# Chunks 3 to 10 of the gelu up-projections as seven block products, with weight sums on VectorE and the residual spilled

## The chip, the cores and the metric

The kernel runs on one core of a Trainium2 chip, as one launch. The metric is the device time of one execution in microseconds; less is better. The engines are TensorE (PE, with its weight loads listed as PEld), VectorE (DVE), ScalarE (ACT), GpSimd (POOL) and SyncE (SP); each works through its own queue.

## The reference, cut to what matters

Two layers, each a token mixer (attention, then a gated recurrence) and a gated feed-forward network, with an RMS norm before and after each and the result added to the residual. The sequence has 512 tokens, the model 1024 features, the feed-forward network 3072. All tensors are float32. The change concerns the up-projection below.

```python
def conv_ffn(x, w_up, conv_w, conv_b, w_down):
    u = causal_dwconv(x @ w_up, conv_w, conv_b)     # width 3 along the tokens
    g, v = u[..., :D_FF], u[..., D_FF:]
    return (jax.nn.gelu(g, approximate=True) * v) @ w_down

x = x + rms_norm(h, norm_mix_post[layer])
h = rms_norm(x, norm_ffn_pre[layer])
h = conv_ffn(h, ffn_w_up[layer], ...)
x = x + rms_norm(h, norm_ffn_post[layer])
```

## The kernel before

Precision comes from splitting. Each float32 operand is held as two fp32r tiles, `hi` (a rounded copy) and `lo` (what is left over), and a product is three matmul passes: hi with hi, hi with lo, lo with hi (`mm3`, L257). `split` (L148) makes them: ScalarE copies `raw` into `hi`, then VectorE subtracts `hi` from `raw` into `lo`. The activations of a stage lie feature by token in `hT`, a pair of tiles of 128 partitions x 8 feature blocks x 512 tokens.

Weights come through a planner written out by hand. `plan` lists every weight block in the order of use. `load` (L193) has SyncE fetch one block of 1 MB into one of three `raw` buffers; `pump` (L167) cuts a block into two units of 128 output features, splits each in two steps of 512 columns, and stops when eight units are live; `take` hands a unit to the matmuls and `done` releases it. `tick` (L222), called after every tile, lets waiting side work go on and then calls `pump`, with a limit of one unit when six or more are live. Loads are issued only when no cut pieces are left.

The feed-forward network (`ffn`, L591) runs over 12 chunks `j`. A chunk is 256 gelu features and the 256 value features that go with them, four tiles of 128 features x 512 tokens. A tile is 8 feature blocks x 3 passes = 24 matmuls of 512 columns into one PSUM bank (`feat_tiles`, `feat`); chunk 0 runs in halves of 256 tokens, because the last tokens come out of the norm late. Each tile goes to `sink` (L607): `conv` (L594) has ScalarE multiply and add the bias from PSUM, VectorE add the two shifted terms, and then ScalarE does the gelu, or VectorE the product with the gelu tile. The 24 gelu tiles stay in the general pool of 32 tiles of 512 columns (`gen`, L118) until the down-projection (`rows_proj`) splits them as activations.

All engines issue in the order in which the program emits the instructions (L102). So an instruction that waits holds up everything emitted behind it on its engine. Dependencies between engines are found by the framework from the tiles; PSUM tiles are one bank each, eight of them (`psum`, L121).

The residual lies in `x_sb`, 128 partitions x 4 token tiles x 1024, from the first load to the end. The norms at the end of a stage (`postnorm`, `prenorm`) read it and write it; during the 12 chunks of a feed-forward network nothing touches it. `gain` (L133) loads a gain row over all partitions into one of two buffers, on GpSimd's queue.

## Time and profile before

| | us |
|---|---|
| median of three runs | 1455.94 (1455.89 to 1456.03) |
| span of the profiled execution | 1454.0 |
| VectorE busy | 879.8 |
| ScalarE busy | 675.9 |
| first feed-forward network, chunks after the norms of the stage before | 510.5 to 764.3 |
| second feed-forward network, the same | 1063.0 to 1316.8 |

The time of a run is the device's own for the whole execution; the span goes from the first to the last instruction of the one execution that was profiled. In a row of instructions the first number after the bar is the busy time of the group and the second the mean of one in ns, then comes the idle time of the engine just ahead of them and what ended it. Matmuls overlap one another, so the duration of one is longer than the distance to the next. In a row of the chain or the timeline the first number is the start and the second the length. In a row of a stretch come the busy times of PE, PEld, DVE, ACT and POOL with their instruction counts, then the granted clock of TensorE, the share of the DMA engines and the GB/s.

### The profile page before, as it was taken

What the parts mean: (1) busy time and instruction counts of PE and PEld (TensorE: products, weight loads), DVE (VectorE), ACT (ScalarE), POOL (GpSimd) and SP (SyncE); (2) the same over time, 40 slices, a digit from 0 to 9 for tenths busy, and PEclk for the clock granted to TensorE, in tenths of its full rate; (3) what the DMA queues carried; (4) which work ended last, traced back from release to release, by engine and by line L of the source; (5) the groups of instructions that cost most, each with busy time, mean ns of one, the idle gap of its engine ahead of it and who ended that gap; (6) DMA issues with size and microseconds to landing.
All of it is one profiled execution on the core that took longest, in us unless ns stands there. A gap on an engine that the chain in (4) does not pass through costs nothing.

```text
span 1454.0 us, 18793 instructions
## 1 busy us (share of the span) xinstructions
PE 1445.0 (99%) x6861; PEld 1214.4 (84%) x6861; DVE 879.8 (61%) x1955; ACT 675.9 (46%) x1532; POOL 133.9 (9%) x275
## 2 busy tenths in 40 slices
PE   9999999999999999999999999999999999999998
PEld 7888888888888898888888888888898888888886
DVE  6767747474735975555564338769775555564333
ACT  7656636262615553343444335589453434444221
POOL 0340414040402100000000001000100000000000
PEclk9999999999999999999999999999999999999999
DMA  7653637372726343323323322432333233223201
GB/s 225 207 146 109 174 113 208 104 215 97 216 96 211 102 131 100 103 87 102 101 88 116 115 73 88 131 116 84 120 102 116 87 102 102 87 104 128 88 0 58
DMA packets 125364, 172.76 MB, mean 119 GB/s; under 512 B 8736, under 2 KB 102392, under 8 KB 125272
## 3 DMA queue, kind: packets, MB, share of 16 engines
q1 hardware_dynamic: 114280, 145.48, 31.0%
q0 software_dynamic: 10144, 25.04, 5.9%
q8 instruction: 54, 0.88, 0.2%
q10 hardware_dynamic: 848, 1.05, 0.2%
q14 instruction: 38, 0.31, 0.1%
HBM read 156.24 MB, written 15.29 MB: 118 GB/s over the span
## 4 chain that ended last, share of the span: by engine, by line
PE 93%; ACT 4%; DVE 3%; issue 1%; DVEq 0%; ACTq 0%
PE ps L259 55%; PE acc L259 24%; PE v L758 8%; PE v L688 1%; DVE xb L967 1%; PE O L909 1%; PE S L854 1%; PE S L808 1%; DVE wlo L150 1%; ACT sig L988 1%; ACT whi L149 1%; PE O L259 1%; PE tr L341 1%; ACT sig L1007 0%; ACT a L1005 0%
## 5 line engine op out<-in xcount | busy, mean ns | idle before, releaser
L259 PE MATMUL ps<-hT,whi 128*128 128x512 f32 (+1 forms) x2752 | 801.3, 375 | 0.0
L259 PEld LDWEIGHTS ps<-hT,whi 128*128 128x128 f32 x2752 | 503.6, 188 | 91.6
L259 PE MATMUL ps<-hT,wlo 128*128 128x512 f32 (+1 forms) x1376 | 515.3, 374 | 0.0
L150 DVE TENSOR_TENSOR wlo<-raw,whi 128x512 fp32r<-128x512 f32 x360 | 230.8, 686 | 187.2 <-ACT whi L149 187.1
L259 PEld LDWEIGHTS ps<-hT,wlo 128*128 128x128 f32 x1376 | 259.1, 188 | 46.5
L149 ACT ACTIVATE whi<-raw 128x512 fp32r<-128x512 f32 x360 | 204.6, 621 | 135.4 <-PE acc L259 121.0
L600 DVE SCALAR_TENSOR_TENSOR u<-ps,cols,u 128x511 f32<-128x511 f32 x192 | 143.8, 749 | 140.6 <-ACT u L596 137.2
L259 PE MATMUL acc<-whi,ahi 128*128 128x512 f32 x512 | 199.7, 390 | 0.0
L259 PE MATMUL acc<-whi,alo 128*128 128x512 f32 x512 | 199.4, 389 | 0.1
L259 PE MATMUL acc<-wlo,ahi 128*128 128x512 f32 x512 | 199.3, 389 | 0.0
L143 ACT ACTIVATE whi<-raw,first_w 128x128 fp32r<-128x128 f32 (+1 forms) x432 | 146.2, 425 | 56.6 <-PE ps L259 33.9
L596 ACT ACTIVATE u<-ps,cols 128x512 f32<-128x512 f32 x96 | 74.8, 779 | 210.0 <-PE ps L259 210.0
L144 DVE SCALAR_TENSOR_TENSOR wlo<-raw,first_w,whi 128x128 fp32r<-128x128 f32 (+1 forms) x432 | 139.5, 389 | 1.4 <-ACT whi L143 1.3
L259 PEld LDWEIGHTS acc<-whi,alo 128*128 128x128 f32 x512 | 96.1, 188 | 20.5 <-DVE alo L150 0.5
L259 PEld LDWEIGHTS acc<-whi,ahi 128*128 128x128 f32 x512 | 96.1, 188 | 19.8
L259 PEld LDWEIGHTS acc<-wlo,ahi 128*128 128x128 f32 x512 | 96.2, 188 | 19.8
L758 PE MATMUL v<-whi,hT 128*128 128x512 f32 x320 | 102.4, 393 | 0.0
L302 POOL DMA_DIRECT2D turned<-T x36 | 19.6, 547 | 763.4 <-DVE T L296 759.9
L309 POOL DMA_DIRECT2D ft<-turned x144 | 78.7, 554 | 39.6 <-issue 17.7
L758 PEld LDWEIGHTS v<-whi,hT 128*128 128x128 f32 x320 | 60.1, 188 | 12.3
L611 ACT ACTIVATE u<-u 128x512 f32<-128x512 f32 x48 | 30.3, 632 | 80.4 <-DVE u L600 80.4
L758 PE MATMUL v<-wlo,hT 128*128 128x512 f32 x160 | 62.3, 389 | 0.0
(171 smaller groups left out, 1010.7 us busy)
## 6 DMA issues: line engine op xcount, KB each, us to landing
raw<-in_ffn_w_up_dram SPq DMA_DIRECT2D x48, 1024.0 KB
raw<-in_attn_w_qkv_dram SPq DMA_DIRECT2D x67, 512.0 KB
raw<-in_ffn_w_down_dram SPq DMA_DIRECT2D x24, 1024.0 KB
raw<-in_lru_w_in_dram SPq DMA_DIRECT2D x8, 1024.0 KB
turned<-T POOLq DMA_DIRECT2D x28, 256.0 KB, 2.6
ft<-turned POOLq DMA_DIRECT2D x112, 64.0 KB, 5.8
vrows<-v SPq DMA_DIRECT2D x16, 256.0 KB
vp<-vrows SPq DMA_DIRECT2D x16, 256.0 KB
```

Source lines behind the costliest of these rows:

```text
L143: nc.scalar.activation(hi[:, k], raw[:, k], AF.Copy, scale=w)
L144: nc.vector.scalar_tensor_tensor(lo[:, k], raw[:, k], w, hi[:, k].bitcast(F32), op0=ALU.mult, op1=ALU.subtract)
L149: nc.scalar.activation(hi, raw, AF.Copy)
L150: nc.vector.tensor_tensor(lo, raw, hi.bitcast(F32), op=ALU.subtract)
L259: mm(dst, l[a], r[b], start=start and n == 0, stop=stop and n == 2)
L302: nc.gpsimd.dma_start(d, T)
L309: nc.gpsimd.dma_start(t[32 * c : 32 * c + 32].rearrange("j (b x) -> j b x", b=4), d.rearrange("(b j) (c x) -> c j b x", j=32, c=4)[c],)
L341: nc.tensor.transpose(ps[:, k * P : (k + 1) * P], xs[i][:, k * P : (k + 1) * P], ident)
L596: nc.scalar.activation(u, ps, AF.Identity, scale=cc[:, j : j + 1], bias=cc[:, 48 + j : 49 + j])
L600: nc.vector.scalar_tensor_tensor(u[:, d:], ps[:, : S - d], wc, u[:, d:], op0=ALU.mult, op1=ALU.add)
L611: nc.scalar.activation(u, u, AF.Gelu_apprx_tanh)
L758: mm(banks[t], hT[a][:, k, t * P : (t + 1) * P], W[b][:, k % 2, :], start=(k, a, b) == (0, 0, 0), stop=(k, a, b) == (KD - 1, 1, 0),)
```

## The change

In chunks 3 to 10 of both networks the gelu half, a product of 256 output features x 1024 inputs x 512 tokens, is cut in two along each of outputs, inputs and tokens, and done as seven products of half-size blocks instead of eight (Strassen's scheme in Winograd's form). A block product is 128 features x 512 inputs x 256 tokens: 4 feature blocks x 3 passes = 12 matmuls of 256 columns. The sums that the scheme needs are made in four places.

- **Weights.** `w_cols` marks these blocks as `wino`. Instead of two units of 128 features, `summed` makes four units from one raw block, the sums being made in place in `raw` by VectorE (four of 512 columns), the splits being one of 1024 columns for the first three units and one of 512 for the fourth. `pump` takes the gelu and the value block together: one sum, first half of the value block, the four summed units, second half of the value block.
- **Tokens.** `token_sums` runs as side work from chunk 1 on, once per network. GpSimd adds `hi` and `lo` back together for the blocks it needs, VectorE forms four sums, each is split. The eight kept tiles lie in the residual's tile, in the two gain buffers and in four general tiles.
- **Residual.** `token_sums` first sends `x_sb` to DRAM on GpSimd's queue; `x_back` fetches it into the same place at chunk 11.
- **Products.** `seven` runs the seven products (steps 1 to 7) and eight quarters of the two value tiles (a to h, six matmuls of 512 columns each) in the order `5 a 1 3 b c 6 2 d 7 e f 4 g h`. Two PSUM banks hold the running sums in their first 256 columns. ScalarE copies product 5 and the sum after product 3 to SBUF and writes the negative of product 1 over the second bank; VectorE makes the other token half of each output tile by a subtraction into the bank's last 256 columns, after 6 and after 7. `tick` is called after each of the 15 steps.

```diff
+SEVEN = range(3, 11)
-    x_sb = cp.tile([P, 4, D], F32, tag="x_sb", name="x_sb")
+    X = [cp.tile([P, 4, D], F32, tag="x_sb", name="x_sb")]
...
+    def summed(i, raw):
+        a, b, c, d = (raw[:, 4 * k : 4 * k + 4, m * P : m * P + P] for m, k in ((0, 0), (0, 1), (1, 0), (1, 1)))
+        shape = [KD, P]
+        def first(hi, lo):
+            two = [h.rearrange("p (k m) c -> p k (m c)", m=2) for h in (hi, lo)]
+            split(*two, raw[:, 0:4, :])
+            nc.vector.tensor_tensor(a, a, c, op=ALU.add)
+        def second(hi, lo):
+            split(hi, lo, raw[:, :, 0:P])
+            nc.vector.tensor_tensor(b, a, b, op=ALU.add)
+            nc.vector.tensor_tensor(a, a, d, op=ALU.subtract)
+        def third(hi, lo):
+            split(hi, lo, raw[:, :, 0:P])
+        def fourth(hi, lo):
+            split(hi[:, 0:4], lo[:, 0:4], d)
+        def ahead():
+            nc.vector.tensor_tensor(c, c, d, op=ALU.add)
+        return [(None, None, ahead)] + [((i, n), shape, f) for n, f in enumerate((first, second, third, fourth))]
...
     def pump(limit=2):
...
+            if not pieces and i + (i < len(plan) and plan[i][0] == "wino") < state["dma"]:
+                if plan[i][0] == "wino":
+                    (s1, *u), v = summed(i, raws.pop(i)), [
+                        plain(i + 1, j, r) for j, r in enumerate(parts_of("feat", raws.pop(i + 1)))
+                    ]
+                    pieces.extend([s1, v[0], *u, v[1]])
+                    state["cv"] += 2
...
+            while pieces and pieces[0][0] is None:
+                pieces.pop(0)[2]()
...
         for j in range(12):
+            if j == 1:
+                side(token_sums(hT, T))
             if j == 11:
+                x_back()
                 prep(3)
+            if j in SEVEN:
+                seven(hT, T, lambda b, ps: sink(b, ps, j))
+            else:
+                feat_tiles(2, hT, lambda b, ps: sink(b, ps, j), j == 0)
...
+    def x_back():
+        X[0] = cp.tile([P, 4, D], F32, tag="x_sb", name=nm("x_sb"))
+        nc.gpsimd.dma_start(X[0], kept.pop())
...
+    def token_sums(hT, T):
+        d = dp.tile([P, 4, D], F32, name=nm("x_kept"))
+        nc.gpsimd.dma_start(d, X[0])
...
+        yield 1
+        def both(k0, n):
+            o = gen(s="B").rearrange("p (k t) -> p k t", k=2)
+            hi, lo = (h[:, k0 : k0 + 2, n * 256 : n * 256 + 256] for h in hT)
+            nc.gpsimd.tensor_tensor(o, hi.bitcast(F32), lo.bitcast(F32), op=ALU.add)
+            return o
...
+        yield 2
+        for k in range(2):
+            b11, b12, b22, b21 = (B[k, n] for n in ((0, 0), (0, 1), (1, 1), (1, 0)))
+            tt(b11, b11, b12, op=ALU.subtract)
+            tt(b12, b12, b22, op=ALU.subtract)
+            tt(b22, b22, b11, op=ALU.add)
+            tt(b21, b21, b22, op=ALU.subtract)
+            yield 1
+            for n, b in enumerate((b11, b22, b12, b21)):
+                split(homes[2 * n][k], homes[2 * n + 1][k], b)
...
+    def seven(hT, T, sink):
+        i, iv = chunk(), chunk()
+        t = gen(s="part")
...
+        left = {
+            1: (0, pairs(0), block(0, 0), 0), 5: (0, pairs(1), turn(0), 1), 6: (1, row(0), turn(1), 1),
+            2: (1, row(4), block(1, 0), 0), 7: (2, row(0), turn(2), 1), 3: (2, row(4), block(1, 1), 1),
+            4: (3, row(0), turn(3), 1),
+        }
+        def product(n):
+            u, l, r, b = left[n]
+            W = take(i, u)
...
+            for k in range(4):
+                for q, (wa, ha) in enumerate(PASSES):
+                    mm(
+                        y[b][:, 0:256], l(W[wa], k), r(ha, k), start=n in (1, 5) and k == q == 0,
+                        stop=k == 3 and q == 2, skip_group_check=True,
+                    )
...
+        a, c = (lambda: y[0][:, 0:256]), (lambda: y[1][:, 0:256])
+        p5, z = t[:, 0:256], t[:, 256:512]
+        for step in "5a13bc62d7ef4gh":
+            if step in "1234567":
+                n = int(step)
+                product(n)
+                if n == 5:
+                    nc.scalar.activation(p5, c(), AF.Copy)
+                elif n == 1:
+                    done()
+                elif n == 3:
+                    nc.scalar.activation(z, c(), AF.Copy)
+                    nc.scalar.activation(c(), a(), AF.Copy, scale=-1.0)
+                elif n == 6:
+                    nc.vector.tensor_tensor(y[0][:, 256:512], z, c(), op=ALU.subtract)
+                elif n == 2:
+                    done()
+                    sink(0, y[0])
+                elif n == 7:
+                    done()
+                    nc.vector.tensor_tensor(y[1][:, 256:512], c(), p5, op=ALU.subtract)
+                else:
+                    done()
+                    sink(1, y[1])
+            else:
+                n = "abcdefgh".index(step)
+                quarter(n)
+                if n % 4 == 3:
+                    done()
+                    sink(2 + n // 4, v[n // 4])
+            tick()
...
-            w_cols(ffn_w_up[layer], j * 256)
+            w_cols(ffn_w_up[layer], j * 256, kind="wino" if j in SEVEN else "feat")
```

More of the change, by code (lines that the diff above doesn't have):

```diff
@@ L155, with plain, f @@
     sides, first_w, first_y, one = [], [], [], []
+    def plain(i, j, raw):
+        def f(hi, lo):
+            h = raw.shape[1] // 2
+            cuts = [(slice(None), slice(0, h)), (slice(None), slice(h, 2 * h))]
+            if raw.shape[1] == 1:
+                cuts = [(slice(None), slice(0, 1), slice(n, n + 512)) for n in (0, 512)]
+            if plan[i][4] is not None:
+                split_normed(hi, lo, raw, plan[i][4] + (2 * j if plan[i][0] == "value" else 0))
+                cuts = []
+            for c in cuts:
+                split(hi[c], lo[c], raw[c])
+        return (i, j), list(raw.shape[1:]), f
+    def summed(i, raw):
[16 more added lines that the diff above has]
+        return [(None, None, ahead)] + [((i, n), shape, f) for n, f in enumerate((first, second, third, fourth))]
     def parts_of(kind, raw):
@@ L170, in pump @@
             i = state["cv"]
-            if not pieces and i < state["dma"]:
-                pieces.extend((i, j, u) for j, u in enumerate(parts_of(plan[i][0], raws.pop(i))))
-                state["cv"] += 1
-            if pieces and state["live"] < W_UNITS:
-                i, j, raw = pieces.pop(0)
-                hi, lo = (
-                    wp.tile([P] + list(raw.shape[1:]), F32R, tag=t, name=nm("w" + t)) for t in ("hi", "lo")
-                )
-                h = raw.shape[1] // 2
-                cuts = [(slice(None), slice(0, h)), (slice(None), slice(h, 2 * h))]
-                if raw.shape[1] == 1:
-                    cuts = [(slice(None), slice(0, 1), slice(n, n + 512)) for n in (0, 512)]
-                if plan[i][4] is not None:
-                    split_normed(hi, lo, raw, plan[i][4] + (2 * j if plan[i][0] == "value" else 0))
-                    cuts = []
-                for c in cuts:
-                    split(hi[c], lo[c], raw[c])
-                units[i, j] = (hi, lo)
+            if not pieces and i + (i < len(plan) and plan[i][0] == "wino") < state["dma"]:
[6 more added lines that the diff above has]
+                else:
+                    pieces.extend(plain(i, j, r) for j, r in enumerate(parts_of(plan[i][0], raws.pop(i))))
+                    state["cv"] += 1
+            while pieces and pieces[0][0] is None:
+                pieces.pop(0)[2]()
+            if pieces and state["live"] < W_UNITS:
+                key, shape, fill = pieces.pop(0)
+                hi, lo = (wp.tile([P] + shape, F32R, tag=t, name=nm("w" + t)) for t in ("hi", "lo"))
+                fill(hi, lo)
+                units[key] = (hi, lo)
                 state["live"] += 1
@@ L235, in drain, with w_cols @@
             tick()
-    def w_cols(w, c0, normed=False):
+    def w_cols(w, c0, normed=False, kind="feat"):
         if normed:
@@ L241, in w_cols @@
             srcs = [(w[:, c0 : c0 + 256].rearrange("(k p) c -> p k c", p=P), KD)]
-        plan.append(("feat", KD, 256, srcs, 0 if normed else None))
+        plan.append((kind, KD, 256, srcs, 0 if normed else None))
     def w_value(w, *cuts):
@@ L315, in prenorm @@
     def prenorm(t, hT, g, wait):
-        xh, gh = halves(x_sb[:, t, :]), halves(g)
+        xh, gh = halves(X[0][:, t, :]), halves(g)
         xs = [gen(s="xs") for _ in range(2)]
@@ L353, in first_transposed @@
                 ps[:, k % 4 * P : (k % 4 + 1) * P],
-                x_sb[:, t, i * 512 : i * 512 + 512].rearrange("t (p k) -> t k p", k=4)[:, k % 4], ident,
+                X[0][:, t, i * 512 : i * 512 + 512].rearrange("t (p k) -> t k p", k=4)[:, k % 4], ident,
             )
@@ L375, in first_squares @@
             nc.scalar.activation(
-                junk, x_sb[:, t, i * 512 : i * 512 + 512], AF.Square, accum_out=first_ss[i][:, t : t + 1]
+                junk, X[0][:, t, i * 512 : i * 512 + 512], AF.Square, accum_out=first_ss[i][:, t : t + 1]
             )
@@ L409, in postnorm @@
         for i, c in enumerate(at):
-            xc = x_sb[:, t, c]
+            xc = X[0][:, t, c]
             nc.vector.scalar_tensor_tensor(xc, u[i], y, xc, op0=ALU.mult, op1=ALU.add)
@@ L619, in ffn @@
         prep, run = rows_proj(12, act_split(gv), order, post, pre)
+        T = []
         for j in range(12):
+            if j == 1:
+                side(token_sums(hT, T))
             if j == 11:
+                x_back()
                 prep(3)
-            feat_tiles(2, hT, lambda b, ps: sink(b, ps, j), j == 0)
+            if j in SEVEN:
+                seven(hT, T, lambda b, ps: sink(b, ps, j))
+            else:
+                feat_tiles(2, hT, lambda b, ps: sink(b, ps, j), j == 0)
@@ L624, in ffn @@
         return run()
+    kept = []
+    def x_back():
+        X[0] = cp.tile([P, 4, D], F32, tag="x_sb", name=nm("x_sb"))
+        nc.gpsimd.dma_start(X[0], kept.pop())
+    def token_sums(hT, T):
+        assert len(sides) == 1
+        d = dp.tile([P, 4, D], F32, name=nm("x_kept"))
+        nc.gpsimd.dma_start(d, X[0])
+        kept.append(d)
+        homes = cp.tile([P, 4, D], F32R, tag="x_sb", name=nm("T"))
+        homes = [homes[:, n] for n in range(4)]
+        homes += [cp.tile([P, D], F32R, tag="gain", name=nm("T"), bufs=2) for _ in range(2)]
+        homes = [[h[:, 0:512], h[:, 512:1024]] for h in homes]
+        homes += [[gen(F32R, "T") for _ in range(2)] for _ in range(2)]
+        homes = [[h.rearrange("p (k t) -> p k t", k=2) for h in hs] for hs in homes]
+        yield 1
[4 more added lines that the diff above has]
+            return o
+        tt = nc.vector.tensor_tensor
+        B = {}
+        for k in range(2):
+            for n, at in (((0, 0), 2 * k), ((0, 1), 2 * k), ((1, 1), 4 + 2 * k), ((1, 0), 4 + 2 * k)):
+                B[k, n] = both(at, n[1])
+        yield 2
+        for k in range(2):
+            b11, b12, b22, b21 = (B[k, n] for n in ((0, 0), (0, 1), (1, 1), (1, 0)))
[6 more added lines that the diff above has]
+                split(homes[2 * n][k], homes[2 * n + 1][k], b)
+            if not k:
+                yield 1
+        T.extend([homes[2 * n], homes[2 * n + 1]] for n in range(4))
@@ new lines, in seven, with block, turn, pairs @@
+    def seven(hT, T, sink):
+        i, iv = chunk(), chunk()
+        t = gen(s="part")
+        y, v = {}, {}
+        def block(kr, n):
+            return lambda h, k: hT[h][:, 4 * kr + k, n * 256 : n * 256 + 256]
+        def turn(n):
+            return lambda h, k: T[n][h][k // 2][:, k % 2]
+        def pairs(m):
+            return lambda w, k: w.rearrange("p (k m) c -> p k m c", m=2)[:, k, m]
+        def row(k0):
+            return lambda w, k: w[:, k0 + k]
+        left = {
[6 more added lines that the diff above has]
+            W = take(i, u)
+            if b not in y:
+                y[b] = psum()
+            for k in range(4):
[4 more added lines that the diff above has]
+                    )
+        def quarter(n):
+            m, k0 = n // 4, 2 * (n % 4)
+            W = take(iv, m)
+            if m not in v:
+                v[m] = psum()
+            for k in (k0, k0 + 1):
+                mm3(v[m], [w[:, k, :] for w in W], [h[:, k, :] for h in hT], k == 0, k == KD - 1)
+        a, c = (lambda: y[0][:, 0:256]), (lambda: y[1][:, 0:256])
[22 more added lines that the diff above has]
+                    sink(1, y[1])
+            else:
+                n = "abcdefgh".index(step)
[4 more added lines that the diff above has]
+            tick()
@@ L1090, in x_half @@
         c = slice(i * 512, (i + 1) * 512)
-        nc.sync.dma_start(x_sb[:, t, c], x[0, t * P : (t + 1) * P, c])
+        nc.sync.dma_start(X[0][:, t, c], x[0, t * P : (t + 1) * P, c])
     def w_part(i, k0, k1):
```

## The prediction

> **What bounds the kernel now.** I read the page's busy times first, then its chain of waits, then the chain in order of time.

> ```profile
> PE 1445.0 (99%) x6861; PEld 1214.4 (84%) x6861; DVE 879.8 (61%) x1955; ACT 675.9 (46%) x1532; POOL 133.9 (9%) x275
> PE 93%; ACT 4%; DVE 3%; issue 1%; DVEq 0%; ACTq 0%
> 1.47 2.50 PE warm L1083 x5
> 500.13 5.75 PE ps L259 x48
> 510.50 253.77 PE ps L259 x1176
> 764.27 125.12 PE acc L259 x552
> ```

> TensorE is the bound, and in the feed-forward stages it is the only one: 253.77 us of up-projection run on it without a gap. The chain rows give the pace of matmuls, which the duration column doesn't (that is a latency). The 48 of 500.13 are 256 columns wide: 5.75/48 = 0.120 us each. Of the 1176, 120 are the rest of chunk 0's 256-wide ones (14.4 us), so the 1056 of 512 columns take (253.77 - 14.4)/1056 = 0.2267 each. Half the columns cost 0.53 of the time.

> ```profile
> 596.00:618.00 22.00, 22.00 (x99) 18.22 (x98) 12.38 (x18) 8.79 (x15) 0.00 (x0) 1.00 0.29 96
> ...
> L150 DVE TENSOR_TENSOR wlo<-raw,whi 128x512 fp32r<-128x512 f32 x360 | 230.8, 686 | 187.2 <-ACT whi L149 187.1
> L600 DVE SCALAR_TENSOR_TENSOR u<-ps,cols,u 128x511 f32<-128x511 f32 x96 | 71.9, 749 | 137.2 <-ACT u L596 137.2
> L615 DVE TENSOR_TENSOR u<-u,u 128x512 f32<-128x512 f32 x48 | 33.2, 692 | 1.6
> L831 DVE TENSOR_TENSOR plo<-ft,phi 128x256 fp32r<-128x256 f32 x8 | 3.4, 419 | 0.2 <-ACT phi L830 0.2
> ...
> L149 ACT ACTIVATE whi<-raw 128x512 fp32r<-128x512 f32 x360 | 204.6, 621 | 135.4 <-PE acc L259 121.0 <-PE ps L259 14.4
> L596 ACT ACTIVATE u<-ps,cols 128x512 f32<-128x512 f32 x96 | 74.8, 779 | 210.0 <-PE ps L259 210.0
> L611 ACT ACTIVATE u<-u 128x512 f32<-128x512 f32 x48 | 30.3, 632 | 80.4 <-DVE u L600 80.4
> L830 ACT ACTIVATE phi<-ft 128x256 fp32r<-128x256 f32 x8 | 3.3, 409 | 0.7 <-DMA ft<-turned 0.7
> L841 ACT ACTIVATE o<-O 128x512 f32<-128x512 f32 x8 | 4.8, 596 | 21.9 <-PE O L259 21.9
> ```

> The first row, a stretch of about one chunk, shows VectorE busy 12.4 of 22 us and ScalarE 8.8. Their idle time is waiting in order: VectorE's halves of the weights wait for ScalarE's (187 us), the convolution's additions for ScalarE's first product (137 us), the gelu for those additions (80 us). Today TensorE waits for none of it, since every tile has its own bank. One gelu tile and the value tile after it, in order of time:

> ```profile
> 600.68 0.39 PE L259 MATMUL ps<-hT,wlo 128*128 128x512 f32 x1
> ...
> 601.11 0.78 ACT L596 ACTIVATE u<-ps,cols 128x512 f32<-128x512 f32 x1 [1.32 <-PE ps L259]
> ...
> 601.92 1.54 DVE L600 SCALAR_TENSOR_TENSOR u<-ps,cols,u 128x511 f32<-128x511 f32 x2 [1.33 <-ACT u L596]
> ...
> 603.55 0.63 ACT L611 ACTIVATE u<-u 128x512 f32<-128x512 f32 x1 [1.66 <-DVE u L600]
> ...
> 604.09 1.14 ACT L149 ACTIVATE whi<-raw 128x512 fp32r<-128x512 f32 x2
> ...
> 604.74 1.29 DVE L150 TENSOR_TENSOR wlo<-raw,whi 128x512 fp32r<-128x512 f32 x2 [1.28 <-ACT whi L149]
> ...
> 608.93 0.69 DVE L615 TENSOR_TENSOR u<-u,u 128x512 f32<-128x512 f32 x1
> 609.54 0.68 DVE L150 TENSOR_TENSOR wlo<-raw,whi 128x512 fp32r<-128x512 f32 x1
> ```

> Queues run in emission order: ScalarE's split of the next weights stands behind the gelu, which stands behind VectorE's two additions. From the tile's last matmul issued at 600.68 to the last half at 606.03 it is 5.35 us, just inside a tile of 24 x 0.2267 = 5.44.

> **What the change removes on TensorE.** A chunk is now a pair of 48 + 48 matmuls, 21.76 us. The gelu half becomes 7 x 12 = 84 matmuls of 256 columns, 10.06 instead of 10.88 us: 0.82 saved, not an eighth. Over 16 pairs (8 chunks, two layers) that is 13.1 us, all that can be won. One product takes 1.44 us, one quarter of a value tile 1.36, the pair 20.94 if nothing waits.

> **What it adds.** 1024-element operations are not in the trace; from 256 to 512 elements VectorE's time grows by 0.267 us, so 0.686 + 2 x 0.267 = 1.22, and ScalarE's 0.621 + 2 x 0.212 = 1.05. A 256-wide copy out of PSUM is 0.596 - 0.212 = 0.38. VectorE's work for a pair: eight additions 5.99, two products 1.38, value halves 4 x 0.686 = 2.74, the four sums on weights 2.74, the halves of the four summed units 3 x 1.22 + 0.69 = 4.35, two 256-wide combinations 0.84; in all 18.0 us of 20.94, before any waiting. ScalarE: 11.8. That fits as a sum; the order decides.

> **Where the order bites.** Eight units of weights are always ahead, so one unit is split after each release: after step 1 the second summed unit of the next pair, after 2 the third, after d the fourth, after 7 the first value unit, after 4 and h the units of the pair beyond. Thus between product 2 and VectorE's subtraction of step 7 the queues hold a convolution, a gelu, a 1024-wide split, a second convolution, its product and a 512-wide split. Product 4 adds into the bank which that subtraction reads, so TensorE must wait for it; behind product 4 stand g, h and the next pair. From the end of product 2: result and handoff 0.20 (last issue at 600.68 to ScalarE at 601.11 is 0.43, one pace of 0.2267 belongs to the step), convolution on ScalarE 0.81 with handoff (601.11 to 601.92), additions 1.54, handoff 0.09, gelu until the next issue 0.54, ScalarE's split 1.05 + 0.03, VectorE's 1.14 (1.22 less the 0.08 by which two neighbours overlap: 2 x 0.686 - 1.29), second pair of additions 1.55, product 0.61 (608.93 to 609.54), fourth unit 0.60, subtraction 0.42, and the release of TensorE:

> ```profile
> 1007.59 2.49 DVE L150 TENSOR_TENSOR alo<-th,ahi 128x512 fp32r<-128x512 f32 x4
> ...
> 1008.33 0.19 PEld L259 LDWEIGHTS acc<-whi,alo 128*128 128x128 f32 x1 [0.53 <-DVE alo L150]
> ```

> The first of those four ends at 1007.59 + 0.68 = 1008.27, TensorE starts at 1008.33: 0.06. Sum 8.64 us. TensorE has d, 7, e and f to do meanwhile: 3 x 1.36 + 1.44 = 5.52. It waits 3.1 us in every pair.

> The subtraction of step 6 reads product 6's bank and writes into the free half of product 2's. Does product 2 wait for it? If columns are kept apart, 0; if a bank is one thing, 0.20 + 0.42 + 0.06 = 0.68. The nearest rows:

> ```profile
> 213.48 1.95 PE L854 MATMUL S<-qk,qk 128*128 128x128 f32 x16
> ...
> 214.57 0.29 DVE L796 CUSTOM_DVE_ANT_0 L<-S,toe 128x128 f32<-128x128 f32 x1 [3.54 <-PE S L854]
> ```

> Here an idle VectorE reads 128 columns that the first matmul of a row wrote, but starts only 1.09 us after that began, when several later ones into other columns are done. I take the wait, and since VectorE's sums on the second unit end about 10.1 us into the pair (its queue is full from product 4 on: additions to -0.2, value halves to 2.4, additions and product to 4.6, the first unit and its sum to 6.4, ScalarE's split to 7.6, half and two sums to 10.0) and product 6's result is there at 10.04, the price is 0.7.

> [...]

> ScalarE's three copies lie beside quarters: the copy of product 5 has a and 1 to hide in (2.8 us), the two after product 3 end near 8.3 where product 6 would start at 8.4. If that cover goes, 0.4 us a pair.

> **Weights and residual.** The value weights of the next pair load when the fourth unit is split, 4.4 us before use by the order above.

> ```profile
> 600.62 0.37 SPq L199 DMA_DIRECT2D raw<-in_ffn_w_up_dram  x1
> ...
> 601.00:602.00 1.00, 1.00 (x6) 0.84 (x5) 0.08 (x1) 0.78 (x1) 0.00 (x0) 1.00 0.17 52
> 604.00:605.00 1.00, 1.00 (x7) 0.80 (x6) 0.26 (x1) 1.00 (x3) 0.00 (x0) 1.00 0.93 328
> 605.00:606.00 1.00, 1.00 (x6) 0.84 (x5) 1.00 (x2) 0.23 (x1) 0.00 (x0) 1.00 0.02 8
> ...
> gain<-in_norm_ffn_post_dram POOLq DMA_DIRECT2D x2, 512.0 KB, 4.0
> ```

> A load of 1 MB is issued at 600.62 and through at 605.0: 4.4 us. So 0 to 0.5 us a pair; I take 0. The residual's 2 MB out have four tiles (21.8 us) before its tile is overwritten; at 4.0 us for 512 KB they take at most 16. Back, they have the whole first part of the down-projection (125.12 us), on GpSimd's queue ahead of two gains needed as late. Nothing. The token sums (16 operations of 0.69 on VectorE, 8 of 0.62 on ScalarE, 8 additions on GpSimd, which no row prices) fall into chunks 1 and 2, where VectorE has 2 x 9.4 us free: between 0 and 4 us for each layer by how late product 5 of chunk 3 finds them; I take 1.

> **Sum.** A pair: 20.94 + 3.1 + 0.7 = 24.8, 3.0 more than now. 16 pairs 48, token sums 2: span 1454.0 + 50 = 1504. The runs' median lies 1.9 above the span: 1506.

> **Rivals.** *TensorE never waits:* -13 + 2, 1445. For it: VectorE's work is below the floor, 18.0 of 20.94. It decides once 8.64 falls to 5.52, as where the splits came ahead of the gelu and the fourth unit behind the subtraction; the queues are against it. 0.10. *Columns kept apart:* 24.1 a pair, 1495. 0.20. *TensorE slows after each wait:* the first five 512-wide matmuls of the program took 2.50 us where 5 x 0.2267 = 1.13, and no later gap in the trace lasts 3 us. If 1.4 us are lost behind each wait, 22 more: 1528. 0.12. [...] *Loads and copies late too:* 0.5 + 0.4 a pair, 14 more: 1520. 0.13. *The waits only eat the gain:* a chain of 6.3 us, so within 0.2%: 0.04. *Paced by the weight loads* (188 ns each, row below): 84 x 0.188 = 15.8 us, 5.7 more than counted, but most of it in place of the waits: 1512 or so. 0.01, since 48 already ran at 0.120.

> ```profile
> L259 PEld LDWEIGHTS ps<-hT,whi 128*128 128x128 f32 x2752 | 503.6, 188 | 91.6
> ```

> The forecast itself has 0.40, with 1499 to 1513 as its own range. From 1482 (columns apart and one ScalarE split of 1.05 off the chain: 23.0 a pair gives 1478, rounded in) to 1532 (slowed clock and some late copies) about 8 in 10 lie. Measurements of this kernel tell 0.2%, 2.9 us, from no change: faster 0.10, within 0.04, slower 0.86.

> **What would show it.** A TensorE wait of about 3 us in each of the 16 pairs, ended by the 256-wide subtraction that precedes product 4, and one of 0.7 ahead of product 2; 256-wide matmuls at 0.120 between waits; VectorE at 18 of some 25 us; granted clock 1.00. It is wrong if TensorE's rows run on without gaps (then near 1445), if the waits are ended by ScalarE or a load, or if the clock falls behind the waits.

## The result, and the profile after

The changed kernel takes 1540.75 us (median of four runs, 1539.25 to 1542.33) against 1455.91: a ratio of 1.0583, with a 95% interval from 1.0568 to 1.0598. That is 84.8 us slower where 50 were forecast. The profiled execution has a span of 1540.6 and a mean granted clock of 0.985.

From the page after, its busy times and the shares of its chain of waits:

```profile
PE 1462.7 (95%) x7437; PEld 1245.0 (81%) x7437; DVE 992.5 (64%) x2083; ACT 717.4 (47%) x1596; POOL 161.8 (10%) x295
...
PE 62%; DVE 20%; issue 13%; ACT 4%; DMA 1%; POOL 1%; DVEq 0%; ACTq 0%; POOLq 0%
```

TensorE is no longer what ends last throughout; VectorE holds a fifth of the chain (`issue` is time in which the engine waited for nothing that the profile shows). The view of waits, for TensorE's weight loads (us in total, times, longest), says where:

```profile
PEld ps L751 <- DVE ps L784: 54.5, 16, 3.6
PEld ps L751 <- DVE ps L778: 13.4, 16, 0.9
PEld ps L751 <- DVE T L151: 6.3, 2, 3.3
PEld ps L751 <- ACT ps L776: 5.2, 4, 2.9
```

L751 are the block products. L784 is VectorE's subtraction after product 7, for which product 4 waits in all 16 pairs, 3.4 us each. L778 is the one after product 6, for which product 2 waits, 0.84 us each. L151 ends the split of the token sums and L776 is ScalarE's negative copy of product 1: both hold up the first pair of a network. VectorE's queue between the two subtractions, in order of time, one pair of the first network:

```profile
638.39 0.42 DVE L778 TENSOR_TENSOR ps<-part,ps 128x256 f32<-128x256 f32 x1
641.42 1.53 DVE L641 SCALAR_TENSOR_TENSOR u<-ps,cols,u 128x511 f32<-128x511 f32 x2 [2.61 <-ACT u L637]
644.66 1.23 DVE L151 TENSOR_TENSOR wlo<-raw,whi 128x1024 fp32r<-128x1024 f32 x1 [1.71 <-ACT whi L150]
645.80 1.53 DVE L641 SCALAR_TENSOR_TENSOR u<-ps,cols,u 128x511 f32<-128x511 f32 x2
647.36 0.69 DVE L656 TENSOR_TENSOR u<-u,u 128x512 f32<-128x512 f32 x1
647.97 0.69 DVE L151 TENSOR_TENSOR wlo<-raw,whi 128x512 fp32r<-128x512 f32 x1
648.57 0.43 DVE L784 TENSOR_TENSOR ps<-ps,part 128x256 f32<-128x256 f32 x1
```

This is the queue of the prediction, item by item: convolution of step 2 (waiting for ScalarE), the 1024-wide half (waiting behind the gelu), convolution and product of step d, the 512-wide half, and only then the subtraction. From one subtraction to the other it is 10.18 us; the prediction's figures give 10.1. The 1024-wide operation takes 1.23 (1.22 estimated). The matmuls on the two sides of that wait:

```profile
645.71 0.39 PE L300 MATMUL ps<-hT,wlo 128*128 128x512 f32 x1
649.05 0.51 PE L751 MATMUL ps<-T,whi 128*128 128x256 f32 x2 [2.95 <-DVE ps L784]
```

Their starts are 3.34 us apart where the pace is 0.23, so product 4 begins 3.1 us late, though the weight loads' wait, counted from the end of the last load, is 3.4.

What the forecast had left out stands in the stretches after the release of product 4. The last figures are granted clock, DMA share and GB/s:

```profile
649.00:649.50 0.50, 0.45 (x3) 0.45 (x4) 0.50 (x1) 0.00 (x0) 0.00 (x0) 1.00 0.00 0
650.50:651.00 0.50, 0.50 (x4) 0.50 (x3) 0.29 (x1) 0.00 (x0) 0.00 (x0) 0.50 0.92 303
651.00:653.00 2.00, 2.00 (x7) 1.61 (x6) 0.89 (x2) 0.78 (x1) 0.00 (x0) 0.50 1.08 376
653.00:653.50 0.50, 0.50 (x2) 0.39 (x2) 0.50 (x1) 0.00 (x0) 0.00 (x0) 0.56 0.99 238
...
623.45:648.57 25.12, 21.49 (x132) 18.89 (x132) 17.23 (x25) 10.62 (x17) 0.00 (x0) 1.00 0.26 84
648.57:675.16 26.59, 23.04 (x132) 20.23 (x132) 17.32 (x25) 10.62 (x17) 0.00 (x0) 0.94 0.25 79
```

The wait ended at 649.05. One microsecond later the granted clock is 0.50 and stays there for 3.4 us, in which half the matmuls fit. The last two rows are whole pairs, from one subtraction L784 to the next: 25.12 us at full clock, 26.59 with the halved stretch. Over both networks the clock is halved at or behind 11 of the 16 waits; with one at an entry it is halved for 13 times 3.41 us, and 22.2 us of full clock are lost.

### The profile page after: what moved, and what is told of

Its sections match the earlier page's. It is cut to its first block, busy times and chain, and to the rows that moved or that the text cites. A ratio compares the mean times of both kernels' runs of the same rounds, so it can differ in the third digit from the quotient of the medians.

```text
span 1540.6 us, 20250 instructions
## 1 busy us (share of the span) xinstructions
PE 1462.7 (95%) x7437; PEld 1245.0 (81%) x7437; DVE 992.5 (64%) x2083; ACT 717.4 (47%) x1596; POOL 161.8 (10%) x295
## 3 DMA queue, kind: packets, MB, share of 16 engines
q10 hardware_dynamic: 848, 1.05, 0.2%
## 4 chain that ended last, share of the span: by engine, by line
PE 62%; DVE 20%; issue 13%; ACT 4%; DMA 1%; POOL 1%; DVEq 0%; ACTq 0%; POOLq 0%
PE ps L300 25%; PE acc L300 17%; PE ps L751 7%; PE v L928 7%; DVE wlo L151 7%; DVE u L641 6%; ACT whi L150 2%; PE v L858 1%; ACT u L652 1%; ACT u L637 1%; PE O L1079 1%; PE S L1024 1%; PE S L978 1%; DVE T L151 1%; DVE x_sb L452 1%
## 5 line engine op out<-in xcount | busy, mean ns | idle before, releaser
L300 PE MATMUL ps<-hT,whi 128*128 128x512 f32 (+1 forms) x2240 | 655.7, 378 | 0.0
L300 PEld LDWEIGHTS ps<-hT,whi 128*128 128x128 f32 x2240 | 409.5, 192 | 68.8
L300 PE MATMUL ps<-hT,wlo 128*128 128x512 f32 (+1 forms) x1120 | 420.4, 375 | 0.0
L151 DVE TENSOR_TENSOR wlo<-raw,whi 128x512 fp32r<-128x512 f32 (+1 forms) x360 | 271.6, 792 | 208.3 <-ACT whi L150 208.3
L150 ACT ACTIVATE whi<-raw 128x512 fp32r<-128x512 f32 (+1 forms) x360 | 226.9, 679 | 198.1 <-PE acc L300 124.6
L300 PEld LDWEIGHTS ps<-hT,wlo 128*128 128x128 f32 x1120 | 214.1, 191 | 38.5
L751 PE MATMUL ps<-T,whi 128*128 128x256 f32 x512 | 101.6, 296 | 57.4 <-DVE ps L784 47.7
L751 PEld LDWEIGHTS ps<-T,whi 128*128 128x128 f32 x512 | 85.7, 199 | 69.6 <-DVE ps L784 54.5
L751 PE MATMUL ps<-hT,whi 128*128 128x256 f32 x384 | 72.1, 287 | 10.2 <-DVE ps L778 10.1
## 6 DMA issues: line engine op xcount, KB each, us to landing
raw<-in_attn_w_qkv_dram SPq DMA_DIRECT2D x67, 512.0 KB
```

The costliest lines, as they stand in the source:

```text
L150: nc.scalar.activation(hi, raw, AF.Copy)
L151: nc.vector.tensor_tensor(lo, raw, hi.bitcast(F32), op=ALU.subtract)
L300: mm(dst, l[a], r[b], start=start and n == 0, stop=stop and n == 2)
L751: mm(y[b][:, 0:256], l(W[wa], k), r(ha, k), start=n in (1, 5) and k == q == 0, stop=k == 3 and q == 2, skip_group_check=True,)
```

## The experiments

Theory: the order of VectorE's queue makes product 4 wait, and the wait makes the clock fall. Rivals: VectorE simply has too much work, and the clock is a symptom.

**Filling the wait (e1).**

```diff
+        fill = psum("fill")
         for step in "5a13bc62d7ef4gh":
+            if step == "4":
+                for _ in range(12):
+                    mm(fill, hT[0][:, 0, 0:P], hT[0][:, 0, :], start=True, stop=True)
```

> Twelve extra 512-wide matmuls into a bank that nothing reads stand ahead of product 4 in all 16 pairs (12 x 0.2267 = 2.7 of the 3.1 us that TensorE waits there). Theory (the wait is long enough that TensorE's clock is halved behind it in some pairs, 1.5 us lost each time): the wait that is left is about 0.4 us, no stretch has a granted clock below 1.00 behind it, the pairs that took 26.6 us take 25.2 like the others, and the kernel takes about 1541 - 15 = 1526. Rival (the 26.6 us come from weight loads or ScalarE and the clock is only a symptom): no change, 1541, or more by what the extra matmuls delay.

Measured: 1528.09 us (ratio 1.0493, interval 1.0475 to 1.0510), 12.7 less, with 192 more matmuls. The clock is halved for three times 3.41 us only, all at the entry of the networks; six of the seven distances between pairs of the first network are 25.2 to 25.4 us. The seventh is 26.5 at full clock, with waits of 0.74 and 0.76 us for ScalarE's copies in it. The weight loads' waits of this kernel, its L788 being the subtraction after product 7:

```profile
PEld ps L751 <- DVE ps L782: 14.3, 16, 0.9
PEld ps L751 <- DVE ps L788: 10.3, 15, 0.9
```

The wait that is left ahead of product 4 is 0.7 us (0.4 expected). Useless work made the kernel faster: with the wait filled, the lost clock falls from 22.2 to 5.1 us. So the clock falls because of the wait.

**The subtraction ahead of the held-back convolutions (e2).**

```diff
                 elif n == 2:
                     done()
-                    sink(0, y[0])
+                    held.append(lambda: sink(0, y[0]))
...
                     nc.vector.tensor_tensor(y[1][:, 256:512], c(), p5, op=ALU.subtract)
+                    for f in held:
+                        f()
```

The same for the sink of quarter d.

> The two tiles that end at steps 2 and d go to their convolution only after the subtraction of step 7. Theory (product 4 waits because that subtraction stands last in VectorE's queue behind two convolutions, a gelu and two splits): the wait ahead of product 4 falls from 3.1 us to under 0.5, the clock stays at 1.00, and the work moved behind it shows as other waits only as far as VectorE's 18 us and its handoffs do not fit into 21 us: 22 to 24 us a pair, 1465 to 1500 in all. Rival (VectorE has more work than a pair allows, wherever it stands): about 25 us a pair, the same wait in another place, 1525 to 1541.

Measured: 1501.81 us, one run. No wait for L785, this kernel's subtraction after product 7, is left. In their place:

```profile
PEld ps L751 <- ACT part L772: 21.5, 14, 1.6
PEld ps L751 <- DVE ps L779: 14.4, 16, 0.9
PEld ps L751 <- ACT ps L777: 12.6, 14, 1.7
```

The pair is 24.2 us, a little outside the expected 22 to 24, and the time a little above 1500: ScalarE's copies of product 5 (L772) and of product 1 (L777) now come late. The theory's wait is gone, but the rival isn't out yet.

**Less work for VectorE, same order (e3).** The four weight sums are left out; the products take unsummed weights.

> The four sums on weights (a to d, 4 x 0.69 us on VectorE in each pair) are left out, so the products take unsummed weights. Theory (the order between step 2 and step 7 sets the pair, and no sum stands there): the wait ahead of product 4 stays at 3.1 us, the one ahead of product 2 at 0.6 to 0.8, the pair at about 25 to 26.6, the total falls by less than 12 us, most of it at chunk 3. Rival (VectorE's throughput is the bound): 4 x 0.69 = 2.7 us less a pair, 1497.

Measured: 1531.54 us, one run, 9.2 less.

```profile
PEld ps L748 <- DVE ps L781: 54.8, 16, 3.7
PEld ps L748 <- DVE ps L775: 12.7, 16, 0.8
PEld ps L748 <- DVE T L151: 1.7, 2, 0.8
```

Taking 2.7 us of VectorE's work out of every pair leaves the wait ahead of product 4 at 54.8. Only the entry gains: 4.6 us on the token sums, and the wait for the negative copy is gone. The amount of work isn't what makes the pairs long.

**The split ahead of the gelu (e4).** In `sink`, `tick()` is called between the convolution and the gelu in these chunks, instead of behind it.

> In the seven-product chunks the gelu is emitted behind the split of the next weights instead of ahead of it. Theory: the chain from product 2 to the subtraction of step 7 loses gelu and split (about 1.7 us) and gains the delay of the second convolution's first step (0.3), so the wait ahead of product 4 falls from 3.1 to about 1.7 us, too short to halve the clock: 16 x (1.4 + 1.0) = 38 us less, 1503. Rival (throughput of VectorE): no work is taken away, about 1541.

Measured: 1512.54 us, one run; the wait ahead of product 4 falls from 54.5 to 32.6 us in all, 1.96 in 14 pairs and 2.56 in the last of each network. After the 14 short ones the clock stays at 1.00, after the two longer ones it is halved: a weight load takes 0.33 us there where it took 0.19. The chain got shorter, though by less than the 1.4 us expected; that, and waits for the negative copy that grew from 5.2 to 11.6 us, is why 1503 wasn't reached.

**A later start (e5).** `SEVEN = range(4, 11)`.

> The seven products begin one chunk later (chunks 4 to 10), the token sums stay in chunks 1 and 2. Theory (VectorE enters chunk 3 with a backlog from the token sums and the first summed units, so product 5 and product 6 of that chunk wait about 3 us each, once per network, with a slowed clock behind): both waits are gone; with them and two pairs fewer (4.4 us each) the kernel takes 1541 - 12 - 9 - 3 = 1517. Rival (the waits belong to the first seven-product chunk as such, for instance its first use of the token sums): they move to chunk 4, 1541 - 9 = 1532.

Measured: 1519.52 us, one run. The wait for the token sums isn't in the list of waits any more; 2.0 us remain for the negative copy. So most of the entry was a backlog of VectorE from chunks 1 and 2.

**Order alone (e6, e7 with quarter d late, e8 from chunk 4).** All the arithmetic is kept. After the subtraction of step 7 come the two held convolutions, then the split, then gelu and product; the second summed unit is split after the subtraction of step 6; quarter d moves between products 6 and 2.

```diff
-        for step in "5a13bc62d7ef4gh":
+        for step in "5a13bc6d27ef4gh":
...
+                elif n == 7:
+                    nc.vector.tensor_tensor(y[1][:, 256:512], c(), p5, op=ALU.subtract)
+                    ends = [sink(0, y[0]), sink(2, v[0])]
...
+            if step in "62d7e4h":
+                tick()
+            for f in ends:
+                f()
```

Here `sink` does the convolution and returns the gelu or the product, to be called later.

> All arithmetic is kept, only the order of emission changes: the convolutions of steps 2 and d come after the subtraction of step 7, gelu and product with the gelu after the next split, the split of the second summed unit after the subtraction of step 6, and quarter d runs between products 6 and 2. Theory (order, not amount of work, makes the pairs long): no wait over 0.5 us in the pairs after chunk 3, 21 to 21.5 us a pair, so the 13 us that the products save show except for the entry: 1456 - 13 + 12 = about 1455, at most 1462. Rival (VectorE's 18 us and its handoffs need 24 us in any order): 24 us a pair, 1495.

> As e6_reordered, but quarter d stands after product 2 as in the changed kernel, so product 2 follows product 6 at once. Theory (product 2 waits for the subtraction that writes other columns of its bank): a wait of 0.7 to 0.9 us ahead of product 2 in all 16 pairs, 11 to 14 us more than e6_reordered. Rival (that wait in the changed kernel came from a late VectorE, not from the bank): the same time as e6_reordered.

> e6_reordered with the seven products in chunks 4 to 10 only. Theory: no entry wait is left, so 14 pairs at 21 us save 14 x 0.8 = 11 us less a few handoffs: 1445 to 1449, faster than the kernel before. Rival (the token sums cost as much as the products save): 1455 or more.

Measured: 1474.94 us (ratio 1.0133, 1.0117 to 1.0149), 1482.25 with quarter d late (1.0181, 1.0164 to 1.0197), 1467.26 from chunk 4 (1.0076, 1.0058 to 1.0094). The pair falls from 26 to 21.7 us, so the rival falls; but 21.7 is what the pair took before, and all three times are misses: 1474.94 where at most 1462 was expected, and the third where its rival had it. With quarter d late the wait ahead of product 2 is back in all 16 pairs; without that it isn't in the list:

```profile
PEld ps L757 <- DVE ps L783: 12.7, 16, 0.8
```

The net difference is only 7.3 us where 11 to 14 were expected, since the waits for product 5's copy (7.8 for 12.2) and for the subtraction after product 7 (3.2 for 4.9) are shorter there. The 0.8 us a pair that were left over show in the third kernel, in ScalarE's order of time:

```profile
640.83 1.16 ACT L150 ACTIVATE whi<-raw 128x512 fp32r<-128x512 f32 x2 [1.99 <-DMA raw<-in_ffn_w_up_dram]
642.83 0.63 ACT L653 ACTIVATE u<-u 128x512 f32<-128x512 f32 x1 [0.84 <-DVE u L641]
643.37 0.76 ACT L637 ACTIVATE u<-ps,cols 128x512 f32<-128x512 f32 x1
644.03 1.05 ACT L150 ACTIVATE whi<-raw 128x1024 fp32r<-128x1024 f32 x1
644.98 0.37 ACT L778 ACTIVATE part<-ps 128x256 f32<-128x256 f32 x1
```

The value weights land 2 us late, since their buffer is freed by the split of the fourth unit, and the copy of product 5 (L778), for which product 3 waits, stands behind all of it.

**The token additions on VectorE (e9).** In `token_sums` the eight additions use `nc.vector` instead of `nc.gpsimd`.

> The eight additions that put hi and lo of the tokens together again move from GpSimd to VectorE. In the changed kernel six 512-wide subtractions on VectorE take 9.9 us beside GpSimd's additions, 3.7 in the kernel before. Theory (GpSimd's two-input additions slow VectorE's down by more than they relieve it): those six take 3.7 us again, each of the eight additions 0.69 us on VectorE (5.5 in all, less than the 6.2 lost so far), and the waits at the entry of chunk 3 stay as they are or get shorter by less than 1 us: 1536 to 1542. Rival (the additions on GpSimd cost VectorE nothing, the six were late for another reason): VectorE's backlog grows by 5.5 us in each network, waits at the entry longer by that, 1550.

Measured: 1538.48 us, one run. GpSimd and VectorE in the changed kernel, then VectorE in this one:

```profile
507.18 1.30 POOL L698 TENSOR_TENSOR B<-hT,hT 128x512 f32<-128x512 f32 x1
512.43 11.51 POOL L698 TENSOR_TENSOR B<-hT,hT 128x512 f32<-128x512 f32 x7 [3.94 <-DVE hT L387]
...
507.08 1.97 DVE L361 TENSOR_TENSOR xs<-x_sb,gain 128x512 f32<-128x512 f32 x1
...
512.86 9.92 DVE L151 TENSOR_TENSOR wlo<-raw,whi 128x512 fp32r<-128x512 f32 x6
```

```profile
507.11 0.68 DVE L361 TENSOR_TENSOR xs<-x_sb,gain 128x512 f32<-128x512 f32 x1
...
512.17 3.69 DVE L151 TENSOR_TENSOR wlo<-raw,whi 128x512 fp32r<-128x512 f32 x6
```

The same six subtractions take 9.92 us beside GpSimd's additions and 3.69 without. The wait for the token sums goes from 6.3 to 4.0 us, 1.2 for each network, a little more than expected. Where the additions run is worth at most some 2 us, and the changed kernel's own runs spread over 3; it isn't what makes the entry.

**The last two waits (e10, and e11 from chunk 4).** As e6, with the second value tile's sink held until the copy of product 5 of the next pair is issued, and both value units cut after the summed ones.

```diff
-                    pieces.extend([s1, v[0], *u, v[1]])
+                    pieces.extend([s1, *u, *v])
...
                 if n == 5:
                     nc.scalar.activation(p5, c(), AF.Copy)
+                    flush()
```

> e6_reordered with two more changes of order: the second value tile's convolution and the split after it come behind the copy of product 5 of the next pair, and both value units are cut after the four summed ones. Theory (what is left in e6_reordered, 0.8 us a pair ahead of product 3, is ScalarE's copy of product 5 standing behind that convolution and behind a load that lands too late): no wait over 0.2 us in the pairs after chunk 3, 20.95 us a pair, 12 us less than e6_reordered, 1463. Rival (VectorE has reached its limit): 21.7 us a pair, 1475.

> e10_reordered_tail with the seven products in chunks 4 to 10 only. Theory: 14 pairs save 0.8 us each, 11 us, and what the entry still costs is under 6 us for both networks: 1444 to 1452, faster than the kernel before. Rival (entry and token sums eat the gain): 1455 to 1467.

Measured: 1463.41 us (ratio 1.0055, 1.0040 to 1.0070), as expected, and from chunk 4 on 1451.96 (nine runs; ratio 0.9974, 0.9963 to 0.9984): 3.9 us, or 0.26%, faster than the kernel before, though at the upper edge of what was expected. One pair of the latter, from one subtraction after product 6 to the next:

```profile
624.79:645.77 20.98, 20.98 (x134) 18.98 (x133) 16.96 (x24) 11.51 (x18) 0.00 (x0) 1.00 0.32 101
```

TensorE is busy for 20.98 of 20.98 us at full clock, with VectorE at 17.0. The 14 pairs save 14 x 0.78 = 10.9 us; some 7 go to the entry, of which 5.3 are waits for the copy of product 5 in the first pairs.

## Why the prediction was right or wrong

- **The floor**, 0.82 us saved a pair, was right: 20.98 measured in the last kernel, 20.94 reckoned.
- **Product 4 waits behind VectorE's queue**: right in mechanism, place, order and size. 3.1 us were forecast, and by the distance between the matmuls' starts, less one pace, product 4 begins 3.1 us late: 50.3 in all for 49.6.
- **Product 2 waits for its bank**: right for this program. No row of before shows this pair of instructions, and the forecast's choice between 0 and 0.7 was the author's estimate. It is 0.79 us by the matmuls' starts (0.84 of the weight loads), and moving a quarter in between took it away. The last section says what stays open.
- **A pair of 24.8 us**: 25.12 to 25.29 where the clock stayed full. The working of the forecast holds for those pairs to within 0.5 us.
- **The step that failed is the clock**: the forecast's sum has it full behind every wait, and the halved clock was left to a rival with a chance of 0.12. That it stays full behind a wait of 3.1 us was the author's estimate; the runs show it at 5 of the 16 waits. The matmuls waited just the 3.1 us forecast, and at the other 11 the clock was halved: 22.2 us were lost. In the changed kernel 1.84 us of idle matmuls in one step of the clock's grid of 3.413 us were enough (last section). The forecast itself had named a clock that falls behind the waits as a sign of being wrong. That rival's price, 22 us, came out near, but in part by luck: it took 1.4 us behind each of 16 waits, and 1.71 us twelve times at 11 waits and once at an entry made it up. Its time, 1528, was the forecast plus this price.
- **The entry was mis-sized**: 2 us for both networks; the first pairs begin 10.3 us late by the matmuls' starts, 6.2 for the token sums and 4.1 for the negative copy. VectorE had enough free time in chunks 1 and 2 as a sum, but in order it came into chunk 3 late; and the negative copy's cover, 0.1 us in the forecast, was gone in those first pairs. Both waits shrink with the backlog: the weight loads' 6.3 and 5.2 us to 1.7 and none in e3, to none and 2.0 in e5.
- **Loads and ScalarE's copies in the later pairs** cost next to nothing in the changed kernel, as forecast. They became the next bound once the order was mended (e2, e6).

The parts, by the matmuls' starts: -13.1 for the products, 50.3 + 12.6 for the two waits, 10.3 for the entry, 22.2 for the clock: 82.3 of the 86.6 between the two spans. Most of the rest is 0.1 us by which the second matmul behind a wait comes late, 3.8 in all. The 35 us between the forecast and the measured time are the clock (22.2), the entry (8.3), the two waits (2.1) and this delay.

## What to carry to other kernels

Where a scheme makes TensorE depend on small operations of other engines in the middle of its own sequence, count what stands ahead of each in its queue; whether the engine has time left as a sum doesn't tell it. Emit the operations that release TensorE first, and those that only empty a bank behind them: here order alone was worth 77 of the 85 us. A TensorE wait is to be priced with the clock behind it: in e4 the waits that left the matmuls idle for 1.54 us cost only themselves, in the changed kernel those of 2.95 to 3.20 us had a halved clock behind them 11 times of 16.

## What the runs showed of the hardware that was not expected

**GpSimd beside VectorE.** In the changed kernel six 512-wide two-input operations of VectorE beside two-input additions on GpSimd took 1.65 us each (9.92/6), and in e9, without those additions, 0.62 (3.69/6). The additions themselves took 1.64 each (11.51/7), the first one 1.30. Beside that first one a VectorE product took 1.97 us and in e9, without it, 0.68: longer by 1.29, where the addition took 1.30. Why the two slow each other down, no run here shows.

**Two halves of one PSUM bank.** In this program a subtraction that writes the last 256 columns of a bank holds up a product into its first 256: the weight loads wait 13.4 us for it in the 16 pairs, 0.84 each, and 12.7 in e7. With a quarter of another bank between them, in e6, the wait is no longer in the list. The tile that the program gives to the framework is the whole bank, so the wait can be the program's own. Whether the chip itself would need it, no run here shows.
